# Fourteen groups of transposes through word copies, one tick later, in a decoder trunk on one core

## The chip, the core and the metric

The kernel runs on one core of one Trainium2 chip. The metric is the device time of one execution in microseconds (us); lower is better. Below, PE is TensorE's matmul stream, PEld its weight loads, DVE is VectorE, ACT is ScalarE, POOL is GpSimd and SP is SyncE. A transpose here is a matmul of a 128x128 block against an identity matrix; its result lands in PSUM, in banks of 128x512 fp32.

## The reference

Two layers of a decoder trunk over 256 tokens of width 2048: an attention mixer with latent projections (MLA), an MLP, a Mamba-2 mixer (SSM), an MLP, all in fp32. Cut to what matters:

```python
def rms_norm(x, g):
    y = xf * lax.rsqrt(jnp.mean(xf * xf, axis=-1, keepdims=True) + RMS_EPS)
    return y * g

def ssm_mixer(h, ...):                       # 8 groups of 512 channels
    ...
    y = y.reshape(B, S, SSM_D_INNER) * jax.nn.silu(z)
    y = y.reshape(B, S, SSM_GROUPS, SSM_D_INNER // SSM_GROUPS)
    y = y * lax.rsqrt(jnp.mean(y * y, axis=-1, keepdims=True) + RMS_EPS)
    return (y.reshape(B, S, SSM_D_INNER) * norm_g) @ w_out

for i in range(DEPTH):
    h = rms_norm(x, mix_norm_g[i])
    x = x + (mla_mixer(h, ...) if i % 2 == 0 else ssm_mixer(h, ...))
    h = rms_norm(x, mlp_norm_g[i])
    x = x + squared_relu_mlp(h, ...)
```

## The kernel before

All activations are held as two row tiles of 128 tokens (t = 0, 1) in quarters of 512 columns (nb = 0 to 3). To be a left-hand operand of the next matmul, a tile must be transposed. The kernel transposes a 128x512 tile by four PE transposes into one PSUM bank (`transposed`, L306 to L316), and then splits the bank into a rounded half `h` on ACT (L299) and the rest `lo` on DVE (L300); fp32r is the rounded format in which PE runs its large matmuls, and each fp32 product is made of three of them. Weights go the same way: an SP DMA brings 512 KB (`wraw`), ACT writes the rounded half `wh` (L102), DVE the rest `wl` (L103). Loads run six units ahead of PE and conversions three; a unit of an ordinary block is twelve matmuls of 512 columns.

PE's order is written out by hand: its instructions run as they are issued in the program. The order on the other engines comes from a planner, which fills each engine's queue by the order in the program and its own estimate of when operands are ready; every engine then runs its queue in order. What is to be put between matmuls is queued with `later(n, fn)`; `tick()` runs at the end of each weight key (24 matmuls in an ordinary block) and runs what is due. `later(0, fn)` runs at the next tick, `later(1, fn)` at the one after it.

Two kinds of places matter here:

- **Boundaries.** `finalize` (L382 to L403) adds a quarter of the residual (L399), multiplies it by the next norm's gain into a scratch tile `xg` (L401), squares it for the norm on ACT (L296), and queues the transposes of both row tiles with `later(0, ...)`. It is called for four quarters each after attention, after the first MLP and after the SSM. `by_tile` is true after attention and after the SSM.
- **Gated y.** In the SSM, `z_block(g)` makes the gate of group g from its matmuls; `gate` then multiplies on POOL (L1322), squares on ACT, makes the norm's factor (POOL, L283), writes the gated y of both row tiles into the scratch tiles `ws[t]` (DVE, L1328), and queues the eight transposes with `later(1, ...)`. Around them stand the group's products `y` on PE (L1291), which POOL (L1294, L1296) and DVE (L1297) take up, and `across` (L1243), a matmul of another group that uses the same two PSUM banks `sm` as the transposes.

Scratch tiles (`scratch()`, pool `s2`) share seven buffers. The MLPs already transpose most of their hidden tiles in the rounded form: `hidden` (L549 on) lets a POOL DMA copy the first three blocks of a tile into a tile `tr` of type fp32r (L559) and hands both to `transposed`, which takes blocks 0 to 2 from the copy with a rounded identity (L313) and block 3 from the fp32 source (L315). The copy leaves the words as they are; the type alone makes PE read them rounded. The rounded identity `identr` is cast on POOL at the start of each MLP from the identity in the tile of constants `cst`.

Of the kernel before, what the change touches and what calls it, by code (L numbers as in the profile page):

```python
# [20 lines left out]
F32 = mybir.dt.float32  # L21
F32R = mybir.dt.float32r
# [6 lines left out]
P = 128  # L29
# [9 lines left out]
NEG = -1.0e30  # L39
MAGIC = 12582912.0  # L40

C_ID, C_G0, C_GQ, C_GK, C_MQ, C_TRI, C_SEL = 0, 128, 144, 336, 528, 656, 784
C_INV, C_DTB, C_ALOG, C_CW, C_CB, C_END = 848, 880, 944, 1008, 1200, 1248


def inv_two_pi_parts():
# [168 lines left out]
class Trunk:  # L215
# [82 lines left out]
    def split_out(self, h, lo, src):  # L298
        self.nc.scalar.activation(h, src, AF.Copy)  # L299
        self.nc.vector.tensor_tensor(lo, src, h.bitcast(F32), ALU.subtract)  # L300

    def transposes(self, src, h, lo, t, wide=True):

        sl = slice(t * P, (t + 1) * P)
        self.transposed(src, h[:, :, sl], lo[:, :, sl], wide)

    def transposed(self, src, h, lo, wide=True):
        b = self.bank(wide)
        src, words = src if isinstance(src, tuple) else (src, None)
        for j in range(4):  # L310
            v = slice(j * P, (j + 1) * P)
            if words is not None and j < 3:
                self.nc.tensor.transpose(b.bitcast(F32R)[:, v], words[:, v], self.ident_r)  # L313
            else:
                self.nc.tensor.transpose(b[:, v], src[:, v], self.ident)  # L315
        self.split_out(h, lo, b.rearrange("p (k n) -> p k n", k=4))  # L316
# [67 lines left out]
    def finalize(self, nb, accs, wide=True):  # L384
        nc = self.nc
        g = self.gain_tile(self.nx_gain[nb])
        if not self.by_tile:
            self.nx[nb] = (self.ktile(self.xtp), self.ktile(self.xtp))
        elif nb % 2 == 0:
            for t in range(2):  # L390
                self.nx[nb // 2, t] = [self.ktile(self.xtp).rearrange("p a b -> p (a b)").rearrange("p (k n) -> p k n", n=P)
                                       for _ in range(2)]
        for t in range(2):
            if self.by_tile:
                h, lo = (v[:, 4 * (nb % 2):4 * (nb % 2) + 4] for v in self.nx[nb // 2, t])
            else:
                h, lo = (v[:, :, t * P:(t + 1) * P] for v in self.nx[nb])
            x = self.x[t][nb]
            nc.vector.tensor_tensor(x, accs[t], x, ALU.add)  # L399
            xg = self.scratch()  # L400
            nc.vector.tensor_tensor(xg, x, g, ALU.mult)  # L401
            self.square_sum(x, self.nx_ssq[:, t * 4 + nb:t * 4 + nb + 1])
            self.later(0, lambda h=h, lo=lo, xg=xg: self.transposed(xg, h, lo, wide))  # L403

    def boundary_end(self):

# [20 lines left out]
    def start(self, seq):  # L427
        nc, d = self.nc, self.d
        self.flow = Flow(nc, self.wp, seq, (6, 3))
        cst = self.c.tile([P, C_END], F32, name="cst")  # L430
        self.cst = cst
        self.ident = cst[:, C_ID:C_ID + P]
        self.mhalf = self.c.tile([P, 16], F32, name="mhalf")
        warm = self.s2.tile([P, 512], F32R, tag="s2", name="warm")
        nc.vector.memset(warm.bitcast(F32), 1.0)
        bank = self.sm.tile([P, 512], F32, tag="sm", name="warmed")
        for _ in range(WARM):
            nc.tensor.matmul(bank, warm[:, :P], warm, start=True, stop=True)
        nc.gpsimd.memset(self.mhalf, -0.5)
        nc.scalar.dma_start(cst[:, C_G0:C_GQ], d["cst"][:, C_G0:C_GQ])  # L440
        nc.scalar.activation(self.stat(1), self.mhalf[:, :1], AF.Copy)
        raws = [self.ktile(self.k4, F32) for _ in range(4)]
        parts = [(0, slice(k, k + 1)) for k in range(4)] + [(1, slice(0, 2)), (1, slice(2, 4)), (2, slice(0, 4)), (3, slice(0, 4))]

        def some_x():
            j, k = parts.pop(0)
            nc.sync.dma_start(raws[j][:, k], d["xT"][j][:, k])

        self.flow.load(2, ((0, 512), (512, 1024)), some_x)
        for u in range(3, 7):  # L450
            some_x()
            self.flow.load(u)
        self.pos = self.c.tile([P, 2], I32, name="pos")
        self.x = [[self.res.tile([P, 512], F32, name=f"x{t}{n}") for n in range(4)] for t in range(2)]

        self.rs_pool = [self.c.tile([P, 4], F32, name=f"rs{i}") for i in range(2)]
        self.phase = 0
        self.xT = [(self.ktile(self.xtp), self.ktile(self.xtp)) for _ in range(4)]

        def split_x(j, ks):  # L460
            h, lo = self.xT[j]
            for k in ks:
                g = cst[:, C_G0 + 4 * j + k:C_G0 + 4 * j + k + 1]
                if (j, k) == (0, 0):
                    nc.vector.tensor_scalar(h[:, k], raws[j][:, k], g, None, ALU.mult)
                else:
                    nc.scalar.activation(h[:, k], raws[j][:, k], AF.Copy, scale=g)
                nc.vector.scalar_tensor_tensor(lo[:, k], raws[j][:, k], g, h[:, k].bitcast(F32), ALU.mult, ALU.subtract)  # L468

        split_x(0, (0,))  # L470
        self.flow.convert(1)
        split_x(0, (1, 2))
        self.flow.convert(2)
        split_x(0, (3,))
        self.flow.load(7)
        nc.sync.dma_start(cst[:, :C_G0], d["cst"][:, :C_G0])
        nc.sync.dma_start(cst[:, C_GQ:], d["cst"][:, C_GQ:])
        nc.sync.dma_start(self.pos, d["pos"])
        split_x(1, range(4))
        ssq = self.stat(8)  # L480
        self.later(0, lambda: split_x(2, range(4)))
        self.later(1, lambda: split_x(3, range(4)))

        def stats(n):
            for t in range(2):
                nc.sync.dma_start(self.x[t][n], d["x"][t * P:(t + 1) * P, n * 512:(n + 1) * 512])
                self.square_sum(self.x[t][n], ssq[:, t * 4 + n:t * 4 + n + 1])
            if n == 3:
                self.set_rstd(ssq)

        for n, at in enumerate(X_AT):
            self.later(at, lambda n=n: stats(n))
# [51 lines left out]
    def mlp_body(self, mp, layer, gain):  # L544
        nc = self.nc
        xa, rs = self.xT, self.rs
        us = {}
        self.ident_r = mp.tile([P, P], F32R, name="identr")
        nc.gpsimd.tensor_copy(self.ident_r, self.ident)  # L549

        def hidden(r, pp, j, t):

            nc.scalar.activation(r, r, AF.Square)
            if (pp, j) not in us:
                us[pp, j] = (self.ktile(self.k4), self.ktile(self.k4))
            h, lo = us[pp, j]
            if pp in WORDS:
                q = mp.tile([P, 384], F32R, tag="tr", name=self.name("tr"), bufs=4)
                nc.gpsimd.dma_start(q.bitcast(F32), r[:, :384])  # L559
                r = (r, q)  # L560
            return lambda wide: self.transposes(r, h, lo, t, wide)

        def relu(src, t):
# [14 lines left out]
        at = [0.0, 0.0]  # L578
# [10 lines left out]
        def turn(r, p, j, t, us):  # L589

            fn = hidden(r, p, j, t)
            at[1] = max(at[0] + us + (COPY if p in WORDS else 0), at[1] + TR_GAP)
            due.append((at[1], lambda: fn(False)))

        def pair_of_banks(pool):
# [49 lines left out]
        for tok in tokens:  # L645
            key = (tok[0], layer) + tok[1:]
            if tok[0] == "s":
                _, p, name, d = tok
# [3 lines left out]
                if count.setdefault(name, 0) % 4 == 0:  # L652
                    pool = self.sm if name == "N7" else self.acc
# [7 lines left out]
            elif tok[0] == "c":  # L661
                _, p, j, o = tok
# [11 lines left out]
            else:  # L674
                _, p, nb, o = tok
# [373 lines left out]
    def ssm_body(self, sp, dp, gain):  # L1049
# [12 lines left out]
        xg = [None] * GROUPS  # L1062
# [241 lines left out]
        def z_block(g):  # L1304
# [11 lines left out]
            def gate():  # L1316
                if g not in ready:
                    self.later(0, gate)
                    return
                for t in range(2):  # L1320
                    x = xg[g][t]
                    nc.gpsimd.tensor_tensor(x, ws[t], x, ALU.mult)  # L1322
                    self.square_sum(x, ssq[:, t:t + 1], scale=rs[t])
                rr = self.rsqrt(ssq, 2, 512, 4 * EPS)
                r = self.stat(2)
                nc.vector.tensor_tensor(r, rr, rs2, ALU.mult)
                for t in range(2):
                    nc.vector.scalar_tensor_tensor(ws[t], xg[g][t], r[:, t:t + 1], ng, ALU.mult, ALU.mult)  # L1328
                    self.later(1, lambda t=t: self.transposes(ws[t], yT[g][0], yT[g][1], t, False))
                self.later(1, lambda: gated.add(g))  # L1330

            self.later(1, gate)

# [4 lines left out]
        for step in SSM_ORDER:  # L1338
# [18 lines left out]
            else:  # L1357
# [12 lines left out]
HEAD_BACKLOG = 4  # L1370
SSM_ORDER = ["B0", "d0", "C0", "x0", "B1", "x1", "C1", "x2", "z0", "x3", "z1", "x4", "z2", "o0", "x5", "z3", "x6", "z4", "o1",
             "x7", "z5", "z6", "o2a", "z7", "o2b", "o3"]


B12 = "raw"
# [1 line left out]
LATE5 = ()  # L1377
TR = (10, 8, 7, 7, 5)
TR_GAP = 4
WORDS = range(1, 7)  # L1380
COPY = 8
PAUSE = 2.7


# [192 lines left out]
```

## Time and profile before

| | us |
|---|---|
| median of 3 runs | 2288.92 |
| lowest and highest run | 2287.88, 2289.85 |
| the profiled execution, time | 2289.32 |
| the profiled execution, span of its trace | 2287.5 |

The span goes from the first to the last instruction; the time has 1.8 us around it. The profile gives busy time and share of the span for each engine, the granted PE clock in tenths for 40 slices of the span, and the chain of work that ended last. Views in order of time give start (us from the span's start), duration, engine, line of the kernel, operation, the tile written and the tiles read, the shapes, and how many instructions a row merges; a bracket holds the engine's idle time before the row and what ended it. PE's durations overlap, since matmuls are pipelined: the distance between starts is what a matmul costs in the stream. A view by tile gives, for each group, the least, median and largest duration in ns. A view of windows gives busy time of PE, PEld, DVE, ACT and POOL with the number of instructions, then PE's clock, the busy share of the DMA engines and GB/s.

### The profile page before, as it was taken

The page shows a single profiled execution, that of the slowest core. Times are in us where ns is not written, and L with a number is a line of the kernel's source. Part 1 is how long each engine was busy: PE and PEld are TensorE (multiplying, and loading weights), DVE is VectorE, ACT ScalarE, POOL GpSimd, SP SyncE. Part 2 cuts the span into 40 slices and gives each one's busy share as a digit, 9 for nine tenths or more (in the row PEclk, how much of TensorE's full clock was granted, in tenths as well). Part 3 has the DMA queues.
Part 4 walks back from the last instruction along what each step waited for, and adds up shares of the span by engine and source line. Part 5 has one row for each costly group of instructions (what it writes and reads, how often), then busy time and mean ns, then how long its engine had stood idle before and what let it go on. Part 6 is the DMA issues. An engine that isn't in the chain of part 4 may idle for free.

```text
span 2287.5 us, 30624 instructions
## 1 busy us (share of the span) xinstructions
PE 2280.0 (100%) x10929; PEld 1893.7 (83%) x10929; DVE 1906.0 (83%) x2318; ACT 1391.2 (61%) x1947; POOL 243.0 (11%) x279
## 2 busy tenths in 40 slices
PE   9999999999999999999999999999999999999999
PEld 7898888888888888888888888888888888888887
DVE  7785698999898897687888688676989989989985
ACT  7775476566566666564666555544666666666663
POOL 1430000000000000000133112110000000000000
PEclk9999999999999999999999999999999999999999
DMA  8435678888888878667877777666688888888875
GB/s 316 151 125 152 202 228 266 261 257 267 265 253 259 268 231 271 202 207 241 279 270 261 251 265 259 221 200 202 208 266 240 267 269 253 261 277 244 267 230 161
DMA packets 164985, 547.52 MB, mean 239 GB/s; under 512 B 18448, under 2 KB 27600, under 8 KB 163808
## 3 DMA queue, kind: packets, MB, share of 16 engines
q1 hardware_dynamic: 151264, 502.44, 66.4%
q0 software_dynamic: 11168, 38.85, 9.0%
q10 hardware_dynamic: 2400, 4.27, 0.5%
q8 instruction: 86, 1.41, 0.2%
q14 instruction: 67, 0.55, 0.1%
HBM read 529.65 MB, written 6.41 MB: 234 GB/s over the span
## 4 chain that ended last, share of the span: by engine, by line
PE 95%; DVE 2%; DMA 2%; ACT 1%; issue 1%; POOL 0%; SPq 0%; ACTq 0%; DVEq 0%
PE acc L330 13%; PE acc L331 13%; PE acc L334 13%; PE yp L606 9%; PE yp L607 9%; PE yp L605 9%; PE st L606 7%; PE st L607 7%; PE st L605 7%; DMA wraw<-mi 1%; PE sm L315 1%; DVE wl L103 1%; PE y L1291 1%; PE acc L607 1%; PE acc L605 1%
## 5 line engine op out<-in xcount | busy, mean ns | idle before, releaser
L102 ACT ACTIVATE wh<-wraw 128x1024 fp32r<-128x1024 f32 (+1 forms) x818 | 856.7, 1053 | 582.3 <-PE acc L331 287.9
L103 DVE TENSOR_TENSOR wl<-wraw,wh 128x1024 fp32r<-128x1024 f32 (+1 forms) x818 | 983.3, 1219 | 230.8 <-ACT wh L102 221.8
L605 PE MATMUL yp<-wh,k 128*128 128x512 f32 x896 | 349.3, 390 | 0.0
L607 PE MATMUL yp<-wh,k 128*128 128x512 f32 x896 | 349.1, 390 | 0.0
L606 PE MATMUL yp<-wl,k 128*128 128x512 f32 x896 | 348.9, 389 | 0.0
L330 PE MATMUL acc<-wh,xt 128*128 128x512 f32 x704 | 279.2, 397 | 1.0 <-ACT wh L102 1.0
L331 PE MATMUL acc<-wh,xt 128*128 128x512 f32 x704 | 274.6, 390 | 0.3 <-DVE xt L468 0.3
L102 ACT ACTIVATE wh<-wrx 128x1024 fp32r<-128x1024 f32 x168 | 177.8, 1058 | 153.7 <-PE yp L607 102.9
L103 DVE TENSOR_TENSOR wl<-wrx,wh 128x1024 fp32r<-128x1024 f32 x168 | 204.1, 1220 | 36.4 <-ACT wh L102 35.5
L606 PEld LDWEIGHTS yp<-wl,k 128*128 128x128 f32 x896 | 168.2, 188 | 35.1 <-DVE wl L103 0.4
L607 PEld LDWEIGHTS yp<-wh,k 128*128 128x128 f32 x896 | 168.2, 188 | 35.1
L605 PEld LDWEIGHTS yp<-wh,k 128*128 128x128 f32 x896 | 168.3, 188 | 34.7
L330 PE MATMUL acc<-wh,k 128*128 128x512 f32 x496 | 196.6, 396 | 0.0
L331 PE MATMUL acc<-wh,k 128*128 128x512 f32 x496 | 193.2, 390 | 0.0
L334 PE MATMUL acc<-wl,xt 128*128 128x512 f32 x704 | 188.3, 389 | 0.0
L605 PE MATMUL st<-wh,xt 128*128 128x512 f32 x448 | 177.4, 396 | 0.0
L607 PE MATMUL st<-wh,xt 128*128 128x512 f32 x448 | 174.9, 390 | 0.0
L606 PE MATMUL st<-wl,xt 128*128 128x512 f32 x448 | 174.9, 390 | 0.0
L330 PEld LDWEIGHTS acc<-wh,xt 128*128 128x128 f32 x704 | 132.2, 188 | 29.8 <-ACT wh L102 1.9
L331 PEld LDWEIGHTS acc<-wh,xt 128*128 128x128 f32 x704 | 132.3, 188 | 28.5 <-issue 1.2
L334 PEld LDWEIGHTS acc<-wl,xt 128*128 128x128 f32 x704 | 132.2, 188 | 27.6
L334 PE MATMUL acc<-wl,k 128*128 128x512 f32 x496 | 132.7, 389 | 0.0
(311 smaller groups left out, 3399.4 us busy)
## 6 DMA issues: line engine op xcount, KB each, us to landing
wraw<-mi SPq DMA_DIRECT2D x256, 512.0 KB, 5.5
wraw<-mo SPq DMA_DIRECT2D x256, 512.0 KB, 5.4
wraw<-si SPq DMA_DIRECT2D x160, 512.0 KB, 4.9
wraw<-so SPq DMA_DIRECT2D x64, 512.0 KB, 4.8
wrx<-mi SPq DMA_DIRECT2D x56, 512.0 KB, 5.1
wrx<-mi POOLq DMA_DIRECT2D x56, 512.0 KB, 7.6
wraw<-wo SPq DMA_DIRECT2D x32, 512.0 KB, 4.2
taps<-xD SPq DMA_DIRECT2D x16, 768.0 KB, 8.6
```

The source lines that it names most:

```text
L102: self.last = nc.scalar.activation(h[:, v], raw[:, v], AF.Copy)
L103: self.last_lo = nc.vector.tensor_tensor(lo[:, v], raw[:, v], h[:, v].bitcast(F32), ALU.subtract)
L315: self.nc.tensor.transpose(b[:, v], src[:, v], self.ident)
L330: nc.tensor.matmul(accs[t][:, :n], ah, wh[:, q, :], start=first and kt + q == 0, stop=False)
L331: nc.tensor.matmul(accs[t][:, :n], al, wh[:, q, :], start=False, stop=False)
L334: nc.tensor.matmul(accs[t][:, :n], lhs(kt + q, t)[0], wl[:, q, :], start=False, stop=en and q == nk - 1)
L605: nc.tensor.matmul(b, ah, wh, start=first and q == 0, stop=False)
L606: nc.tensor.matmul(b, ah, wl, start=False, stop=False)
L607: nc.tensor.matmul(b, al, wh, start=False, stop=last and q == 1)
L1291: nc.tensor.matmul(y[t][c, o], part(t)[:, c], xg[g][t][:, o], start=True, stop=True)
```

## The change

A helper `words` copies the first n blocks of a scratch tile by a POOL DMA into another buffer (of the MLP's pool in the MLPs, else of the scratch pool), and `transposed` takes as many blocks from the copy as there are. It is now also used for the gated y of every group other than group 5 (`SOON`), and at boundaries for quarters with `nb < 3 - by_tile`: 0 and 1 after attention and after the SSM, 0 to 2 after the first MLP. Both row tiles of such a group are copied, four blocks for t = 0 and three for t = 1, and the transposes (and the mark that the group is gated) run one tick later. Seven of the eight blocks are so transposed in rounded form; that makes the results of these transposes less exact. The rounded identity is made once at the start from an input of its own. In the MLPs the same tiles are copied as before.

```diff
-C_ID, C_G0, C_GQ, C_GK, C_MQ, C_TRI, C_SEL = 0, 128, 144, 336, 528, 656, 784
+C_G0, C_GQ, C_GK, C_MQ, C_TRI, C_SEL = 0, 16, 208, 400, 528, 656
...
+    def words(self, src, n, pool=None):
+
+        if pool:
+            q = pool.tile([P, n * P], F32R, tag="tr", name=self.name("tr"), bufs=4)
+        else:
+            q = self.s2.tile([P, 512], F32R, tag="s2", name=self.name("tr"))[:, :n * P]
+        self.nc.gpsimd.dma_start(q.bitcast(F32), src[:, :n * P])
+        return src, q, n
...
     def transposed(self, src, h, lo, wide=True):
         b = self.bank(wide)
-        src, words = src if isinstance(src, tuple) else (src, None)
+        src, words, n = src if isinstance(src, tuple) else (src, None, 0)
         for j in range(4):
             v = slice(j * P, (j + 1) * P)
-            if words is not None and j < 3:
+            if j < n:
                 self.nc.tensor.transpose(b.bitcast(F32R)[:, v], words[:, v], self.ident_r)
             else:
                 self.nc.tensor.transpose(b[:, v], src[:, v], self.ident)
...
-            self.later(0, lambda h=h, lo=lo, xg=xg: self.transposed(xg, h, lo, wide))
+            early = nb < 3 - self.by_tile
+            if early:
+                xg = self.words(xg, 4 - t)
+            self.later(int(early), lambda h=h, lo=lo, xg=xg: self.transposed(xg, h, lo, wide))
...
-        self.ident = cst[:, C_ID:C_ID + P]
+        self.ident_r = self.c.tile([P, P], F32R, name="ident")
+        self.ident = self.ident_r.bitcast(F32)
...
-        nc.sync.dma_start(cst[:, :C_G0], d["cst"][:, :C_G0])
+        one = self.scratch()
+        nc.sync.dma_start(one[:, :P], d["one"])
+        nc.gpsimd.tensor_copy(self.ident_r, one[:, :P])
...
-        self.ident_r = mp.tile([P, P], F32R, name="identr")
-        nc.gpsimd.tensor_copy(self.ident_r, self.ident)
...
-            if pp in WORDS:
-                q = mp.tile([P, 384], F32R, tag="tr", name=self.name("tr"), bufs=4)
-                nc.gpsimd.dma_start(q.bitcast(F32), r[:, :384])
-                r = (r, q)
+            if by_words(pp, j, t):
+                r = self.words(r, 3, mp)
...
-                    self.later(1, lambda t=t: self.transposes(ws[t], yT[g][0], yT[g][1], t, False))
-                self.later(1, lambda: gated.add(g))
+                    w = ws[t] if g == SOON else self.words(ws[t], 4 - t)
+                    self.later(1 + (g != SOON), lambda t=t, w=w: self.transposes(w, yT[g][0], yT[g][1], t, False))
+                self.later(1 + (g != SOON), lambda: gated.add(g))
...
+SOON = 5
...
-WORDS = range(1, 7)
...
+def by_words(p, j, t):
+
+    return 0 < p < 7
```

More of the change, by code (lines that the diff above doesn't have):

```diff
@@ L40 @@
 MAGIC = 12582912.0
-C_ID, C_G0, C_GQ, C_GK, C_MQ, C_TRI, C_SEL = 0, 128, 144, 336, 528, 656, 784
-C_INV, C_DTB, C_ALOG, C_CW, C_CB, C_END = 848, 880, 944, 1008, 1200, 1248
+C_G0, C_GQ, C_GK, C_MQ, C_TRI, C_SEL = 0, 16, 208, 400, 528, 656
+C_INV, C_DTB, C_ALOG, C_CW, C_CB, C_END = 720, 752, 816, 880, 1072, 1120
 def inv_two_pi_parts():
@@ L591, in turn @@
             fn = hidden(r, p, j, t)
-            at[1] = max(at[0] + us + (COPY if p in WORDS else 0), at[1] + TR_GAP)
+            at[1] = max(at[0] + us + (COPY if by_words(p, j, t) else 0), at[1] + TR_GAP)
             due.append((at[1], lambda: fn(False)))
@@ L1564 @@
     cw = f(ssm_conv_w)[0].reshape(4, 48, P).transpose(2, 1, 0).reshape(P, 192)
+    a["one"] = np.eye(P, dtype=np.float32)
     a["cst"] = np.ascontiguousarray(np.concatenate([
-        np.eye(P, dtype=np.float32), f(mix_norm_g)[0].reshape(16, P).T, rep(f(mla_qk_norm_q)[0]), rep(f(mla_qk_norm_k)[0]),
+        f(mix_norm_g)[0].reshape(16, P).T, rep(f(mla_qk_norm_q)[0]), rep(f(mla_qk_norm_k)[0]),
         upper * np.float32(NEG), np.triu(one), sel, rep(inv), rep(f(ssm_dt_bias)[0]),
```

## The prediction

> **What bounds the kernel now.** I read the page first, then the chain of waits, then TensorE's order of time around three groups of transposes, then the engines that feed them.
>
> ```profile
> span 2287.5 us, 30624 instructions
> PE 2280.0 (100%) x10929; PEld 1893.7 (83%) x10929; DVE 1906.0 (83%) x2318; ACT 1391.2 (61%) x1947; POOL 243.0 (11%) x279
> PEclk9999999999999999999999999999999999999999
> PE 95%; DVE 2%; DMA 2%; ACT 1%; issue 1%; POOL 0%; SPq 0%; ACTq 0%; DVEq 0%
> ```
>
> TensorE (PE) is busy all the time at the full granted clock, and the chain that ended last is PE for 95%. So a nanosecond taken off PE's own stream comes off the time, unless a new wait takes it back. The question is what a transpose costs in that stream. Three views in order of time, columns start, duration, engine, line, operation: a group of eight fp32 transposes between ordinary matmuls, a group of three rounded ones and one fp32 in the MLP, and the weight loads of both.
>
> ```profile
> 1164.41 1.07 PE L334 MATMUL acc<-wl,xt 128*128 128x512 f32 x4
> 1165.32 1.03 PE L315 MATMUL sm<-cst,s 128*128 128x128 f32 x8
> 1166.11 0.48 PE L330 MATMUL acc<-wh,xt 128*128 128x512 f32 x1
> 1166.66 0.39 PE L330 MATMUL acc<-wh,xt 128*128 128x512 f32 x1
> ...
> 407.53 0.39 PE L606 MATMUL yp<-wl,k 128*128 128x512 f32 x1
> 407.99 0.37 PE L313 MATMUL sm<-identr,tr 128*128 128x128 f32 x3
> 408.20 0.30 PE L315 MATMUL sm<-cst,s 128*128 128x128 f32 x1
> 409.03 0.39 PE L605 MATMUL st<-wh,xt 128*128 128x512 f32 x1
> ...
> 1165.32 0.79 PEld L315 LDWEIGHTS sm<-cst,s 128*128 128x128 f32 x7
> 408.00 0.22 PEld L313 LDWEIGHTS sm<-identr,tr 128*128 128x128 f32 x2
> 408.16 0.14 PEld L315 LDWEIGHTS sm<-cst,s 128*128 128x128 f32 x1
> ```
>
> Durations overlap; starts count. Four ordinary matmuls take 1165.32 - 1164.41 = 0.91 us, 0.227 each. From 1164.41 to 1166.66 is 2.25 us and holds six ordinary ones (1.36): **the eight fp32 transposes add 0.89 us**, 0.109 apart (the seven loads show it: (0.79 - 0.14)/6 = 0.108). From 407.53 to 409.03 is 1.50 us and holds five ordinary ones (1.13): **three rounded and one fp32 add 0.37 us**.
>
> What one more rounded transpose costs is the disputed number. The three start within 0.21 us, before the fourth. But their loads stand further apart than the first starts: two loads of 0.14 us fill 0.22, so the second begins 0.08 after the first, and the next at 408.16 again 0.08 later, while an ordinary matmul before the group hid the first load. In a longer run the load sets the pace: I take 0.083 us. The lower bound is 0.06 (0.21 us for three steps, the last at the load's pace of 0.08 or a little more); the upper bound is fp32's own 0.109.
>
> **The sum.** The diff changes the seven groups of gated y other than `SOON` (eight transposes each) and the quarters with `nb < 3 - by_tile`: two after attention, three after the first MLP, two after the SSM. I count seven quarters, so 14 groups, each now four rounded (t=0), then three rounded and one fp32 (t=1), back to back. One group then adds 0.37 + 4 x 0.083 = 0.70 us instead of 0.89. That saves 0.19 us, **14 x 0.19 = 2.7 us**. At 0.06 it would be 14 x 0.28 = 3.9, at 0.109 14 x 0.08 = 1.2.
>
> The Trainium skill, "TensorE: Matmul & The Clock Gate", section "Back-to-back issue gap", gives about 81 ns per matmul for a stream of loads and matmuls with 128 columns, and 56 ns for isolated matmuls of that width. The loads' 0.08 us side with the first; by it I estimate 14 x 0.20 = 2.8 us, by the second 14 x 0.29 = 4.0 us.
>
> **The copies.** Each group adds two POOL DMAs from SBUF to SBUF, 256 KB and 192 KB, 28 in all. Rows of the copies that the MLPs have already, then the gate of group 0 and the tightest gate, group 3:
>
> ```profile
> L559 POOL DMA_DIRECT2D tr<-s x48: 536/552/590, 364.1 to 2150.1; - x48
> DMA to landing us min/median/max: 2.1/5.1/7.2
> ...
> 1159.47 0.74 DVE L1328 SCALAR_TENSOR_TENSOR s<-xtm,st,gb 128x512 f32<-128x512 f32 x1
> 1159.84 6.25 POOL L1294 TENSOR_TENSOR xtm<-xtm,gb 128x512 f32<-128x512 f32 x2 [2.95 <-PE y L1291]
> 1166.17 1.62 POOL L1296 TENSOR_TENSOR xtm<-xtm,far 128x512 f32<-128x512 f32 x1
> ...
> 1349.49 0.75 DVE L1328 SCALAR_TENSOR_TENSOR s<-xtm,st,gb 128x512 f32<-128x512 f32 x1
> 1352.88 0.81 PE L315 MATMUL sm<-cst,s 128*128 128x128 f32 x6
> ```
>
> Queued behind a copy that waits for its source on POOL are L1294 and L1296, and DVE's L1297 waits for those. In group 0 the second copy would hold L1294 from 1159.84 to about 1160.8, 1 us; its result is next needed by the gate eight ticks later, so I charge 0 for it and let DVE's side of it count with the banks below. A tick in the SSM and at a boundary is one key of 24 matmuls, 24 x 0.227 = 5.44 us. In group 3 the second half of the gated y is ready at 1350.24 and its transposes move from 1352.88 to about 1358.3, so the copy has 8.1 us; group 0 has 1170.8 - 1160.2 = 10.6. An issue (0.55, inside the landing or ahead of it) and a landing of 5.1 fit, and even 0.55 + 7.2 = 7.8 does. `SOON`, group 5, with 2.7 us, is not moved. At the boundaries:
>
> ```profile
> 222.89 1.28 DVE L401 TENSOR_TENSOR s<-x,gb 128x512 f32<-128x512 f32 x2
> 227.16 0.60 PE L315 MATMUL yp<-cst,s 128*128 128x128 f32 x4
> ...
> 229.62 1.28 DVE L401 TENSOR_TENSOR s<-x,gb 128x512 f32<-128x512 f32 x2
> 233.49 0.60 PE L315 MATMUL yp<-cst,s 128*128 128x128 f32 x4
> ```
>
> Sources are ready at 224.17 and 230.90, the moved transposes due at about 232.6 and 238.9: 8.4 and 8.0 us. The other quarters follow the same pattern of two ticks. Hidden too, but with under 1 us to spare at the slowest landing seen: I charge 0 and keep 14 x 0.3 = 4.2 us as its bound. The copies carry 14 x 448 KB = 6.4 MB, 1.2% of what is moved. At the 266 GB/s of the row below that is 24 us of transfer if nothing hid it; the weights are loaded six units of 2.72 us ahead, so I charge nothing.
>
> ```profile
> 1157.00:1179.00 22.00, 22.00 (x155) 17.99 (x154) 19.49 (x31) 13.21 (x27) 9.29 (x4) 1.00 0.81 266
> ```
>
> **Scratch slots.** `words` takes its copy from the seven scratch buffers. At a gate there live at most two sources, two copies, two tanh tiles and one weighted x, seven, and the first source goes when its copy has landed. Where two quarters finish one tick apart (after attention, at the end of the SSM) the first leaves three or four slots taken, and the second wants four and two short-lived ones: it fits with a wait of about a Square (0.6 us) ahead of the last copy. Nothing on PE is due then, charged 0. The identity's move to the start takes one cast off each MLP, off the chain.
>
> **The rivals.**
>
> *The copies stand behind POOL's long products (slower).* POOL runs its queue in order. In group 0 the second source is ready at 1160.21, 0.37 us after L1294 could start. If both L1294 and L1296 are queued ahead of the copy, it issues at 1167.8 and lands at 1172.9 or, at 7.2, 1175.0; PE wants it at 1171.0. Groups 0, 1, 2 and 4 have this neighbour: 4 x 1.9 to 4 x 4.0 = 7.6 to 16 us, net 2294 to 2302. It decides when the issue is later than about 1165.9; one L1294 ahead (to about 1163) is harmless. Against it: in program order the copy comes first. For it: only readiness by the planner's costs, not by these rows, sets the order.
>
> *The banks come free too late (slower or about even).* The views of vector and tensor work behind groups 0 and 2:
>
> ```profile
> 1173.22 1.27 DVE L300 TENSOR_TENSOR k<-sm,k 128x512 fp32r<-128x512 f32 x2
> 1177.09 1.02 PE L1243 MATMUL sm<-s,cb 128*128 128x512 f32 x2
> ...
> 1261.12 1.03 PE L315 MATMUL sm<-cst,s 128*128 128x128 f32 x8
> 1267.10 1.28 DVE L300 TENSOR_TENSOR k<-sm,k 128x512 fp32r<-128x512 f32 x2
> 1270.01 2.35 DVE L103 TENSOR_TENSOR wl<-wraw,wh 128x1024 fp32r<-128x1024 f32 x2
> 1271.98 1.07 PE L334 MATMUL acc<-wl,k 128*128 128x512 f32 x4
> ...
> DVE xtm L1297 <- POOL xtm L1294: 10.7, 7, 2.0
> ```
>
> Both `sm` banks hold a group until L300 has read them; the next user, L1243, comes two ticks after the transposes now and one tick after them with the change. DVE reads group 0's first bank 8.5 us after the transposes start (1173.86 against 1165.32). The same lag from 1170.8 ends at 1179.3, L1243 would wait 2.4 us; group 1 looks like it, group 2 lags 6.6 us (to 1273.2, 0.5 us late), group 4 like it, group 3 less. Sum 5.8 us, net 2292.1, and more if DVE falls back further: it waits in order for POOL's products (last row), which copies can delay by an issue or two of 0.55, and in group 2 a weight half is done at 1271.2, only 0.8 us before PE takes it. Against it: the lag is DVE's backlog up to 1173.2, not the transposes' own, and 1173 is still before the moved L1243.
>
> The Trainium skill, "SBUF — State Buffer", section "A bandwidth-pool intuition that's wrong (but worth ruling out)", speaks against the change: a GpSimd-issued DMA of some 620 ns took some 3100 beside a VectorE copy that held the port they share, since its descriptors waited. The 48 copies here issue in 536 to 590 ns with DVE busy 83%, so the trace shows no sign of it; by that rule I estimate that a pair of copies would be 5 us later and miss the tight ticks.
>
> *The short pace holds (faster).* If rounded transposes go on at 0.06, 3.9 us: 2285.0. *A stall elsewhere goes too:* with 1 us beyond that, 2284. *The change gives nothing:* rounded ones in a long run at fp32's pace and late landings eat the 1.2 us: 2288.9.
>
> **How the numbers follow.** The profiled execution took 2289.32 us for its span of 2287.5; the median is 2288.92 and the runs go from 2287.88 to 2289.85. The sum 2289.32 - 2.7 = 2286.6 in that execution is 2286.3 by the median. Chances: the forecast 40%, the short pace 20%, a stall gone too 7%, banks 16%, POOL's queue 13%, nothing gained 4%. 0.2% is 4.6 us, about what a measurement can tell from no change, so below 2284.3 counts as faster: 7% and two fifths of the short pace, 15%. Above 2293.5: POOL's queue and some of the banks' 16%, 19%. The rest, 66%, is within. The range from 2283.5 to 2294 takes in the short pace and the banks and leaves out most of POOL's queue and a rest at both ends, some 18%; the likeliest case alone is 2285 to 2287.7, from the two bounds of the pace.
>
> **What would show it.** Each step right: L315 falls by 98 transposes, and 98 of the rounded form appear beside the MLPs' 144; a group of eight adds 0.70 us between ordinary matmuls, its loads 0.08 apart; no PE row waits for a DMA of a copy; L1243 starts in step with the matmuls before it. Wrong: loads 0.06 apart (2285); a gap on PE ahead of a group, with the copy's issue behind L1294 or landing after the tick; a gap ahead of L1243 with L300 later than it; new rows in which PE waits for L103 near 1272 and 1412. A span more than 4.6 us off with none of these would mean that the rearranged order of the other engines, not the edits, set it.

## The result and the profile after

| | before | after |
|---|---|---|
| median, us (6 runs each) | 2289.6 | 2303.53 |
| lowest and highest run | 2287.88, 2289.86 | 2300.07, 2306.68 |
| profiled execution, time and span | 2289.32, 2287.5 | 2300.07, 2298.0 |

After against before: 1.0060, 95% interval 1.0049 to 1.0071. The change makes the kernel slower by 14 us; the profiled execution, the fastest of the six, by 10.75. The page of the changed kernel hardly shows why:

```profile
span 2298.0 us, 30746 instructions
PE 2283.8 (99%) x10929; PEld 1892.3 (82%) x10929; DVE 1910.2 (83%) x2318; ACT 1392.9 (61%) x1947; POOL 256.1 (11%) x306
PEclk9999999999999999999999999999999999999999
PE 45%; DVE 1%; ACT 0%; DMA 0%; issue 0%; SPq 0%; DVEq 0%; ACTq 0%
```

PE's busy time rose by 3.8 us with the same 10929 matmuls, 98 of them cheaper, and the span by 6.7 us more than that. So there are waits, and matmuls that last longer. The view of waits of the changed kernel says whose (us in total, times, longest); before had no row like the first:

```profile
PE sm L1254 <- DVE k L300: 7.8, 4, 3.9
PE warmed L451 <- DVE warm L448: 1.4, 1, 1.4
PE acc L343 <- DVE wl L103: 1.0, 2, 0.6
```

L1254 is `across` (L1243 before). The order of time on PE around group 1 of the changed kernel holds all that happened to the forecast:

```profile
1218.07 1.07 PE L343 MATMUL acc<-wl,xt 128*128 128x512 f32 x4
1218.97 0.71 PE L322 MATMUL sm<-ident,tr 128*128 128x128 f32 x7
1219.52 0.29 PE L324 MATMUL sm<-ident,s 128*128 128x128 f32 x1
1219.57 0.48 PE L339 MATMUL acc<-wh,xt 128*128 128x512 f32 x1
1219.89 0.39 PE L340 MATMUL acc<-wh,xt 128*128 128x512 f32 x1
1220.12 0.40 PE L339 MATMUL acc<-wh,xt 128*128 128x512 f32 x1
...
1230.42 2.05 PE L1254 MATMUL sm<-s,cb 128*128 128x512 f32 x2 [3.85 <-DVE k L300]
1231.48 1.42 PE L339 MATMUL acc<-wh,xt 128*128 128x512 f32 x1
1232.69 0.63 PE L340 MATMUL acc<-wh,xt 128*128 128x512 f32 x1
1233.12 0.63 PE L339 MATMUL acc<-wh,xt 128*128 128x512 f32 x1
...
1235.68 1.46 PE L343 MATMUL acc<-wl,xt 128*128 128x512 f32 x4
1236.97 0.40 PE L339 MATMUL acc<-wh,xt 128*128 128x512 f32 x1
```

**The pace is as forecast.** From 1218.07 to 1220.12 are 2.05 us with six ordinary matmuls (1.36): the group adds 0.69 us, where eight fp32 ones added 0.89. In the next matmuls a little of that 0.20 us is made up: from the fourth matmul ahead of a group to the eighth behind it the medians are 3.39 us before and 3.21 after, 0.18 us less, which is 2.5 us in 14 groups. The experiments below reckon with that.

**Then `across` waits 3.85 us for L300**, and after it matmuls start 0.43 us apart instead of 0.227. The window from 1229 to 1237 us of the changed kernel (busy time of PE, PEld, DVE, ACT and POOL, then PE's clock, DMA share, GB/s) shows that the granted clock is 0.57, and two rows of before give the normal length of the same matmuls:

```profile
1229.00:1237.00 8.00, 6.58 (x15) 4.54 (x16) 5.37 (x8) 4.07 (x6) 0.00 (x0) 0.57 0.93 284
```

```profile
1224.65 1.02 PE L1243 MATMUL sm<-s,cb 128*128 128x512 f32 x2
...
1228.28 0.39 PE L330 MATMUL acc<-wh,xt 128*128 128x512 f32 x1
```

From `across` to the first matmul of the next weight unit are 1236.97 - 1230.42 = 6.55 us after, 1228.28 - 1224.65 = 3.63 before: 2.9 us lost to the slow clock. In tenths of full speed over 57 us, as on the page, it does not show.

**The account.** PE's last matmul ends 10.6 us later than before; with the 2.5 us gained, 13 us were lost on balance. The losses lie between 1170 and 1440 us, where PE goes from 1.4 us ahead of the kernel before to 11.4 behind it. Waits of `across` 7.8 (four: groups 0, 1, 2 and 4, with 1.4, 3.9, 1.7 and 0.9), slow clock 2.9, waits for weight halves 1.0 make 11.7. Most of the rest lies around the waits: over each of them the starts are some 0.17 us further apart than the idle time and one matmul, and the next two starts 0.07 us or more. Why L300 is late, VectorE's order of time shows, first of the changed kernel (group 0, then group 1), then of `e5_words_on_time` below, which transposes group 0 at the old tick and stands here for the old order:

```profile
1171.81 2.18 DVE L1287 SCALAR_TENSOR_TENSOR mt<-mt,dt,cb 128x128 f32<-128x128 f32 x8
1173.91 2.35 DVE L103 TENSOR_TENSOR wl<-wraw,wh 128x1024 fp32r<-128x1024 f32 x2
1176.18 1.28 DVE L300 TENSOR_TENSOR k<-sm,k 128x512 fp32r<-128x512 f32 x2
...
1225.22 2.18 DVE L1287 SCALAR_TENSOR_TENSOR mt<-mt,dt,cb 128x128 f32<-128x128 f32 x8
1227.32 2.35 DVE L103 TENSOR_TENSOR wl<-wraw,wh 128x1024 fp32r<-128x1024 f32 x2
1229.60 1.28 DVE L300 TENSOR_TENSOR k<-sm,k 128x512 fp32r<-128x512 f32 x2
```

```profile
1172.86 1.28 DVE L300 TENSOR_TENSOR k<-sm,k 128x512 fp32r<-128x512 f32 x2
1174.06 2.18 DVE L1287 SCALAR_TENSOR_TENSOR mt<-mt,dt,cb 128x128 f32<-128x128 f32 x8
1176.15 2.35 DVE L103 TENSOR_TENSOR wl<-wraw,wh 128x1024 fp32r<-128x1024 f32 x2
```

At the old tick L300 stands ahead of eight products of the heads (L1287, 2.18 us) and two weight halves (2.35 us); a tick later the planner puts it behind them. The transposes moved by a tick (5.4 us), `across` did not. Before the change `across` of group 0 started 3.2 us after L300 had read the first bank. In the changed kernel L300 has read it 7.5 us after the group's first transpose starts, against 8.6 before. So the lag gave back 1.1 us of the 5.4, the margin of 3.2 us is used up, and `across` waits. In groups 1, 2 and 4 the lag itself grew, from 8.6, 6.7 and 6.8 us to 11.3, 8.1 and 7.1.

### The profile page after: what moved, and what is told of

Same layout as the page of the kernel before. It is cut to its first block, busy times and chain, and to the rows that moved or that the text cites. A ratio compares the mean times of both kernels' runs of the same rounds, so it can differ in the third digit from the quotient of the medians.

```text
span 2298.0 us, 30746 instructions
## 1 busy us (share of the span) xinstructions
PE 2283.8 (99%) x10929; PEld 1892.3 (82%) x10929; DVE 1910.2 (83%) x2318; ACT 1392.9 (61%) x1947; POOL 256.1 (11%) x306
## 5 line engine op out<-in xcount | busy, mean ns | idle before, releaser
L102 ACT ACTIVATE wh<-wraw 128x1024 fp32r<-128x1024 f32 (+1 forms) x818 | 857.9, 1054 | 581.2 <-PE acc L340 276.5
L103 DVE TENSOR_TENSOR wl<-wraw,wh 128x1024 fp32r<-128x1024 f32 (+1 forms) x818 | 985.3, 1221 | 235.6 <-ACT wh L102 224.2
L102 ACT ACTIVATE wh<-wrx 128x1024 fp32r<-128x1024 f32 x168 | 178.0, 1059 | 152.8 <-PE yp L618 97.0
L103 DVE TENSOR_TENSOR wl<-wrx,wh 128x1024 fp32r<-128x1024 f32 x168 | 204.4, 1221 | 38.2 <-ACT wh L102 37.0
L339 PEld LDWEIGHTS acc<-wh,xt 128*128 128x128 f32 x704 | 133.3, 189 | 29.4 <-ACT wh L102 1.0
L616 PE MATMUL st<-wh,sN 128*128 128x512 f32 x336 | 133.0, 396 | 0.0
```

The lines of the kernel that those rows point to most:

```text
L102: self.last = nc.scalar.activation(h[:, v], raw[:, v], AF.Copy)
L103: self.last_lo = nc.vector.tensor_tensor(lo[:, v], raw[:, v], h[:, v].bitcast(F32), ALU.subtract)
L339: nc.tensor.matmul(accs[t][:, :n], ah, wh[:, q, :], start=first and kt + q == 0, stop=False)
L616: nc.tensor.matmul(b, ah, wh, start=first and q == 0, stop=False)
```

## The experiments

All times are medians; ratios are against the kernel before on the same chip, with 95% intervals. Differences are against the changed kernel unless said otherwise.

**`across` a tick later.**

```diff
-                self.later(1, across)
+                self.later(2, across)
```

> The changed kernel with one number altered: the product `across` is queued two ticks after its weighted x instead of one, so it again stands two ticks behind the transposes that were moved. Theory A (the loss is `across` waiting for the two `sm` banks until VectorE's L300 has read them, plus the slower clock after the longest of these waits): the gaps of 1.76, 4.25, 2.08 and 1.28 us ahead of L1254 go or fall below 0.5 us each, the clock stays at 1.00 throughout, and the time falls by about 12 us to 2286-2290 us. Rival B (the copies, by POOL, the SBUF or VectorE's delay, slow the SSM and L1254 only shows it): the waits move to another instruction and the time stays at 2297-2304 us. Rival C (the backlog of VectorE is the limit, and whatever is due next on PE waits): part is won, 2292-2297 us, with waits for the products' y or for `far` instead.

Measured 2292.52 us, ratio 1.0013 (1.0004 to 1.0022). No PE row waits for L300 any more, but one new wait stands near 1204 us, for a weight half, with a granted clock of 0.50 until 4.8 us after it:

```profile
PE acc L343 <- DVE wl L103: 2.2, 1, 2.2
```

Theory A was right on the gaps and too hopeful on the time. The time is in rival C's range, though the wait is not for what rival C named.

**Boundaries alone.** The gates go back to fp32 transposes at the old tick without copies.

> The seven gates are put back as before (fp32 transposes, one tick after the gate, no copies); the seven boundary quarters keep the changed form. Theory A (the loss is in the SSM's gates alone, and the boundaries give 0.18 us a group): 7 x 0.18 = 1.3 us faster than before, 2287-2289 us, and no gap ahead of `across`. Rival B (the boundaries' copies or later transposes cost something too, hidden under the gates' loss): 2290-2293 us, with PE waits of the next stage's first matmuls for L300 at 298, 885 or 1620 us.

Measured 2289.02 us, 0.9995 (0.9986 to 1.0004), no wait of `across`. The loss is in the gates; the boundaries' gain, forecast as 1.3 us, is inside what can be told from nothing.

**The late tick without copies.** The gates' transposes are fp32 from their source, a tick later; the boundaries are as before.

```diff
-            early = nb < 3 - self.by_tile
+            early = False
...
-                    w = ws[t] if g == SOON else self.words(ws[t], 4 - t)
+                    w = ws[t]
```

> No copies and no rounded transposes at all: the gates' transposes stay fp32 from their source but come one tick later as in the changed kernel; the boundaries are as before. Theory A (the tick alone makes the loss): gaps ahead of L1254 for groups 0, 1, 2 and 4 like the changed kernel's, and 2297-2306 us, since the 2.5 us of the faster pace are missing too. Rival B (the copies make the loss): no gaps, 2288-2291 us.

Measured 2305.89 us, 1.0070 (1.0056 to 1.0084), with the same row of waits as the changed kernel:

```profile
PE sm L1254 <- DVE k L300: 7.8, 4, 3.9
PE acc L343 <- DVE wl L103: 3.7, 4, 1.2
```

The tick alone makes the loss. The changed kernel, with copies and rounded transposes, is about 2.4 us faster than this one, near the 2.5 of the pace, but the intervals of the two (1.0049 to 1.0071 and 1.0056 to 1.0084) overlap.

**The gates' transposes in `acc` banks.**

> The changed kernel, but the gates' moved transposes go to banks of the ring `acc` (those of the blocks' accumulators) and leave the two `sm` banks alone. Theory A (the two `sm` banks are what `across` waits for): no gap ahead of L1254; the time is 2286-2290 us, if the blocks do not then wait for `acc`. Rival B (copies): unchanged, 2297-2304 us. Rival C (VectorE's backlog limits through any bank): a block's first matmul waits for L300 on an `acc` bank in place of L1254, and the time is 2292-2304 us.

Measured 2311.53 us, 1.0089 (1.0074 to 1.0104). `across` waits no more, but the transposes themselves wait for their banks, 8.6 us for the residual's additions (L436) and 3.1 us for L1214, which read the blocks' sums out of `acc`; a block's matmul also waits 1.4 us for L300, as rival C had it. A miss: the new waits cover what the move takes away, so the run decides little between the theories.

**Copies, but the old tick.** Groups 0, 1, 2, 4 and 7, whose sources are ready early enough, use copies and rounded transposes at the old tick; 3, 5 and 6 stay fp32.

```diff
-                    w = ws[t] if g == SOON else self.words(ws[t], 4 - t)
-                    self.later(1 + (g != SOON), lambda t=t, w=w: self.transposes(w, yT[g][0], yT[g][1], t, False))
-                self.later(1 + (g != SOON), lambda: gated.add(g))
+                    w = self.words(ws[t], 4 - t) if g in EARLY else ws[t]
+                    self.later(1, lambda t=t, w=w: self.transposes(w, yT[g][0], yT[g][1], t, False))
+                self.later(1, lambda: gated.add(g))
...
-SOON = 5
+EARLY = (0, 1, 2, 4, 7)
```

> The changed kernel without the tick at the gates: all gates' transposes are queued one tick after the gate, as before; groups 0, 1, 2, 4 and 7, whose sources are ready 5 us and more before that tick, use word copies and the rounded form, groups 3, 5 and 6 stay fp32. The boundaries are as in the change. Theory A (the tick, not the copies, makes the loss): L300 keeps its place ahead of the heads' products on VectorE, no gap ahead of L1254, and 12 groups gain 0.18 us each: 2286.5-2288.5 us. Rival B (the copies slow POOL, VectorE or the loads): 2291 us or more, with waits for L103 or L300. Rival C (the copies land too late for the early tick): PE waits at L322 for the copies' DMA, some us in all, 2289-2296 us.

Measured 2287.15 us, 0.9992 (0.9983 to 1.0001): 1.8 us under the kernel before, where 12 groups of 0.18 make 2.2. No PE wait for a copy or ahead of `across`. It is the fastest kernel of the study; by the interval it is not shown to be faster than before. It shows that the tick was not needed for most groups: the copies of its gates and last boundary land in 2.9 us in the median, at most 4.9, and in the kernel before group 0 had 5.1 us from its source to its transposes.

**Copies that nothing reads**, with fp32 transposes at the old tick.

> The seven gates issue their copies, but nothing reads them: the transposes are fp32 from the source at the old tick. The boundaries are as in the change. Theory A (copies cost nothing): as with the gates put back, 2288-2290 us, no gap ahead of L1254. Rival B (copies slow the SSM by themselves): 2293-2300 us.

Measured 2288.78 us, 0.9997 (0.9988 to 1.0006). That is what the boundaries alone gave (0.9995): the copies cost nothing that can be measured.

**The heads' products behind L300** in VectorE's queue.

```diff
-                nc.vector.scalar_tensor_tensor(half(t), half(t), dt[:, t, h:h + 1], cb[g][:, 256 * t:256 * t + P],
-                                               ALU.mult, ALU.mult)
+                with self.tc.issue_after(self.cut.ins):
+                    nc.vector.scalar_tensor_tensor(half(t), half(t), dt[:, t, h:h + 1], cb[g][:, 256 * t:256 * t + P],
+                                                   ALU.mult, ALU.mult)
```

> The changed kernel, with one edge in VectorE's queue: the heads' products (L1287 of the change) are queued behind the L300 that was issued last ahead of them. Theory A (what makes L300 late is the work that stands ahead of it in VectorE's queue, eight products of 2.18 us and two weight halves of 2.35): L300 moves ahead of most products, the four gaps shrink by 1 to 2.2 us each, the one of 4.25 us below 2.5 and with it the stretch at the slow clock; 2292-2298 us. Rival B (L300 is late because its own bank or ACT's half is late, not for its place): the gaps stay and the time is 2300 us or more.

Measured 2306.17 us, 1.0074 (1.0060 to 1.0088). The waits of `across` did shrink, from 7.8 us to 4.7 (group 0's is gone, the longest is 1.8), and that step of theory A holds. The time did not follow: waits for weight halves rose from 1.0 us to 9.0 (6.4 on L103, 2.6 on L102). The forecast was wrong, and this is the first sign of a second cause.

**Group 1 put back** (fp32, old tick).

> The changed kernel with group 1's gate alone put back (fp32, old tick, no copy). Theory A: of the loss only group 1's part goes, 4.0 us of waiting and, if the slow clock behind it belongs to the long wait, 3.1 us more: 2303.5 - 7.1 + 0.2 = 2296.6 us; the gaps of groups 0, 2 and 4 stay at 1.3 to 2.1 us. Rival (the slow clock has another cause): 2299.5 us, or the slow stretch turns up behind another gap of under 2.5 us. Rival (the waits share one backlog, so that taking one away lengthens the next): 2300 us or more.

Measured 2299.62 us, 1.0043 (1.0029 to 1.0057), 3.9 less than the changed kernel where 7.1 were forecast. Group 1's gap is gone, those of 0, 2 and 4 stay; new ones came, 3.6 us for weight halves (L103) and 1.2 us for the gated y itself (L1339). The time and the trace are as the first rival had them: the slow clock turned up behind group 2's wait of 1.7 us, which follows a wait of 1.5 us. Taking the long wait away does not take the slow clock away.

**One `sm` bank left free.** Of the gates' two banks one comes from the ring `yp`.

```diff
-                    self.later(1 + (g != SOON), lambda t=t, w=w: self.transposes(w, yT[g][0], yT[g][1], t, False))
+                    self.later(1 + (g != SOON), lambda t=t, w=w: self.transposes(w, yT[g][0], yT[g][1], t, g != SOON))
```

> The changed kernel, but of the two banks of a gate's transposes one comes from the ring `yp` (that of the products y) and one from `sm`, so that one of the two `sm` banks stays free for `across`. Theory A (`across` waits only because both `sm` banks are held): the gaps ahead of L1254 vanish or stay under 0.5 us although L300 runs as late as in the change, and 10 us or so come back: 2289-2295 us, with what is left in waits for weight halves (L103). Rival B (VectorE's lateness costs the same in any case): the wait moves to another first user of a bank (L1302 or L1254) or of a weight half, 2298 us or more.

Measured 2299.15 us, 1.0043 (1.0029 to 1.0057). Its view of waits:

```profile
PE acc L343 <- DVE wl L103: 6.4, 5, 1.8
PE acc L339 <- ACT wh L102: 3.8, 4, 1.5
```

Every wait of `across` is gone although L300 is as late as ever, so the held banks are the cause of those waits. But 10.2 us stand at weight halves instead: rival B is right on the sum. The banks are only the first thing that VectorE's lateness meets. How much is met next differs: with `across` later, where no bank is waited for either, only one wait of 2.2 us for a weight half came up. No run shows why it is so much more here.

**Group 1 alone, then group 0 alone, a tick later**, all else as in `e5_words_on_time`.

> The kernel with word copies and the old tick at the gates (groups 0, 1, 2, 4 and 7 in the rounded form), with group 1's transposes alone a tick later. It was 2287.2 us without that tick. Theory A1 (each group's wait is its own): a gap of about 4 us ahead of L1254 near 1224 us and 3 us at the slow clock behind it, 2294 us. Theory A2 (the long wait of group 1 in the change was built up by group 0's late tick ahead of it): a gap of 1.5 to 2.5 us, no slow clock, 2289-2290 us.

> The same with group 0's transposes alone a tick later. Theory A1: a gap of 1.5 us ahead of L1254 near 1175 us and nothing else, 2288.7 us. Theory A2 (group 0's tick also disorders what follows): beside the 1.5 us waits for weight halves (L103) near 1204 to 1224 us that the kernel before does not have, 0.5 to 2.6 us, in all 2289.5-2292 us.

Measured 2292.96 us (1.0014, 1.0005 to 1.0024) and 2295.15 us (1.0026, 1.0015 to 1.0036). Each has a gap of 1.3 us at its own `across`; group 1's wait of 3.9 us at `across` and the slow clock behind it are absent, so they were built up behind group 0's late tick (A2). But each costs 6 to 8 us against 2287.15, more than A2 allowed, and most of it later: group 0's tick makes group 1's transposes wait 2.7 us for their copy, whose source is late, with a granted clock of 0.50 until 3.9 us after it, and group 1's costs a wait of 2.1 us for a weight half near 1274 us. What happens in between, the queues of SP, ScalarE and VectorE, one after the other, show, first of `e5_words_on_time` and then of `e11_only_group0`:

```profile
1173.34 0.45 SPq L1280 DMA_DIRECT2D cm<-cumD  x1
1173.88 0.42 SPq L390 DMA_DIRECT2D gb<-sng  x1
1174.35 0.93 SPq L1280 DMA_DIRECT2D cm<-cumD  x2
1177.39 1.47 SPq L85 DMA_DIRECT2D wraw<-si  x2
...
1188.60 1.25 ACT L1322 ACTIVATE s<-acc,rs 128x512 f32<-128x512 f32 x2
...
1189.87 1.28 DVE L1323 SCALAR_TENSOR_TENSOR s<-s,acc 128x512 f32<-128x512 f32 x2
```

```profile
1172.47 0.42 SPq L1280 DMA_DIRECT2D cm<-cumD  x1
1172.99 0.47 SPq L390 DMA_DIRECT2D gb<-sng  x1
1175.33 1.46 SPq L85 DMA_DIRECT2D wraw<-si  x2
1176.89 0.92 SPq L1222 DMA_DIRECT2D taps<-xD  x2
1179.97 3.20 SPq L85 DMA_DIRECT2D wraw<-si  x3
1183.21 1.02 SPq L1280 DMA_DIRECT2D cm<-cumD  x2
...
1191.27 0.99 ACT L1284 ACTIVATE mt<-cm,pcum 128x128 f32<-128x128 f32 x3 [4.61 <-DMA cm<-cumD]
...
1194.17 1.25 ACT L1322 ACTIVATE s<-acc,rs 128x512 f32<-128x512 f32 x2
...
1192.60 1.36 DVE L1287 SCALAR_TENSOR_TENSOR mt<-mt,dt,cb 128x128 f32<-128x128 f32 x4 [4.68 <-ACT mt L1285]
...
1195.44 1.28 DVE L1323 SCALAR_TENSOR_TENSOR s<-s,acc 128x512 f32<-128x512 f32 x2
```

The planner moved two loads of the heads' rows `cm` behind five weight loads in SP's queue, from 1174.35 to 1183.21 us. ScalarE then waits 4.61 us for them in order, with a weight half and the next gate's tanh (L1322) behind, and VectorE 4.68 us for ScalarE. The gate's work comes 5.6 us later, and VectorE has idle time where it had work before. ScalarE does not wait longer for `cm` in all: from 1150 to 1450 us it is 24.3 us in the first kernel and 24.7 in the second (25.8 before the change, 25.4 after). What changed is where the wait falls: VectorE's waits for the heads' exponentials rose from 2.3 to 5.6 us (from 1.3 to 5.1 with the change). Its busy time from 1180 to 1200 us, from the view of windows, tells the kernels with group 0's late tick from those without, all but the last of the table:

| kernel | VectorE busy, us of 20 |
|---|---|
| before; copies at the old tick | 18.11; 18.69 |
| group 1 alone late (group 0 at the old tick) | 18.24 |
| changed; group 0 alone late | 12.40; 12.20 |
| `across` later; one `sm` bank free; heads' products behind | 10.90; 11.46; 13.80 |
| below, `cm` by POOL: changed; with one `sm` bank free | 14.31; 17.25 |

With group 1 alone late the dip comes one group later: 12.70 us from 1220 to 1240, where `e5_words_on_time` has 17.20. So the disorder follows the moved transposes. But it does not set the time by its size: `across` later has the least in the table, 10.90, and took 2292.52 us.

**`cm` loaded by POOL's queue**, in the changed kernel, with one `sm` bank free as well, and as a control with the copies at the old tick.

```diff
-            nc.sync.dma_start(cm, cumD[h:h + 1].to_broadcast([P, S]))
+            nc.gpsimd.dma_start(cm, cumD[h:h + 1].to_broadcast([P, S]))
```

> The changed kernel with the heads' rows of cumulated sums (cm) loaded by POOL's DMA queue instead of SP's, so that they no longer stand behind weight loads. Theory A3 (the late tick does its harm by two ways, the two sm banks and cm loads that come late behind weight loads on SP): ScalarE's waits for cm fall, the waits for weight halves near 1204 us go, group 0's gap at `across` of about 1.5 us stays, groups 1 and 2 fall to about that too; 2293-2297 us. Rival (VectorE's backlog is general and cm is only where it shows): 2300 us or more.

> The changed kernel with both: one bank of the gates' transposes from `yp`, and cm loaded by POOL. Theory A3: neither way of harm is left; no gap ahead of L1254, VectorE's wait for the heads' exponentials under 3 us in all, no PE waits for weight halves between 1200 and 1290 us; 2286-2290 us. Rival (general backlog): waits for weight halves stay, 2296 us or more.

> The control: the kernel with word copies at the old tick (2287.2 us) with cm loaded by POOL. If that move neither helps nor harms by itself, 2286-2289 us; if POOL's long products delay cm there, 2290 us or more, and the two runs beside it cannot be read as tests of SP's order.

Measured 2307.03 us (1.0070, 1.0051 to 1.0088), 2290.44 us (1.0005, 0.9996 to 1.0015) and 2295.11 us (1.0027, 1.0016 to 1.0038). With both, the late tick costs no more than can be told from nothing, though the time is 0.4 us above the forecast range: `across` does not wait, and weight halves cost PE 2.0 us in the whole span. The views of waits, first with `cm` alone moved, then with both:

```profile
PE sm L1254 <- DVE k L300: 10.0, 4, 3.5
```

```profile
PE acc L343 <- DVE wl L103: 1.3, 2, 1.0
PE acc L339 <- ACT wh L102: 0.7, 1, 0.7
```

With `cm` alone moved, the waits of `across` grew from 7.8 to 10.0 us and ScalarE's waits for `cm` did not fall (29.4 us from 1150 to 1450): the first forecast failed, and the bank wait stands by itself. The control was not neutral, 8 us slower than without the move, with 5.2 us of waits for weight halves near 1271 and 1416 us; loading by POOL has a price of its own and another order. By the control's own condition the other two cannot be read as tests of SP's order.

What stands is this. With the bank freed alone some 10 us of loss remained, with `cm` moved alone some 18, and with both none that can be told from nothing. So a kernel with all late ticks need not lose time, and the held banks are one part of the loss. That the other part is VectorE's disorder fits the traces, but is argued; that the position of `cm` on SP is its source is not shown.

## Why the prediction was wrong

**Right.** The pace: 0.70 us for a group was forecast, 0.69 measured. The page of the Trainium skill "TensorE: Matmul & The Clock Gate", section "Back-to-back issue gap", has 81 ns per matmul for a stream of loads and matmuls with 128 columns. In the 14 groups the seven rounded transposes start 0.076 us apart, near that and above the 0.06 of the short pace. The copies: charged 0, and with copies that nothing read no cost showed. POOL's queue as a rival: false. This view of POOL in the changed kernel shows both copies of group 0 ahead of L1305 (L1294 before), and groups 1, 2 and 4 have the same order:

```profile
1158.20 0.63 POOL L308 DMA_DIRECT2D tr<-s  x1 [2.75 <-issue]
1159.35 0.54 POOL L308 DMA_DIRECT2D tr<-s  x1 [0.52 <-DVE s L1339]
1159.91 4.76 POOL L1305 TENSOR_TENSOR xtm<-xtm,gb 128x512 f32<-128x512 f32 x2
```

Every copy of the changed kernel issued in 538 to 798 ns with VectorE busy 83%, so no issue looks like the 3100 ns of the Trainium skill's "SBUF — State Buffer", section "A bandwidth-pool intuition that's wrong (but worth ruling out)".

**The step that failed** is the one that counted a tick as time for the copy and as nothing else. The sum held no term for what the tick does to the two `sm` banks; that stood among the rivals with 16%. The runs show what that term is worth: `across` waits 7.8 us for L300 and matmuls at the slow clock behind the longest wait cost 2.9 us, and the same row of waits comes with the tick alone, without copies. The rival had place and mechanism right. It took L300's lag as fixed and so had 2.4, 2.4, 0.5 and 0.5 us for groups 0, 1, 2 and 4, 5.8 in all; measured are 1.4, 3.9, 1.7 and 0.9. What it held against itself was wrong: "the lag is DVE's backlog up to 1173.2, not the transposes' own" supposes that L300 keeps its place in VectorE's queue and is done at about 1173. It lost that place to 4.5 us of other work and started at 1176.18.

Two terms were missing altogether: the slow clock, and the idle time that a changed order in SP's, ScalarE's and VectorE's queues makes. In the changed kernel the second shows as 1.0 us at weight halves and, since group 1's wait is 3.9 us here and 1.3 with group 1 alone late, in the length of that wait; in the experiments it surfaces as late weight halves tens of us on. The prediction's last sentence named that kind of cause only for a span that none of its signs would explain.

**Open** is why the planner places `cm` later when only a gate's transposes move, and how much of the loss this move alone makes; since the control was not neutral, no run separates it from other shifts of order.

## What to carry to other kernels

Work moved by a slot on a busy engine takes its readers along: before charging zero for it, find who reads its result, what that reader stands behind in its in-order queue at the new time, and who needs the buffer next. Where a planner orders the other engines, compare their queues before and after, loads included; a small load that is moved behind large ones can idle an engine that has no time to spare. And check first that the delay is needed: here five of the seven moved groups had time for the copy at the old tick.

## What the runs showed of the hardware

A wait on PE costs more than itself once it is long. Of eleven PE waits of 2.2 us and more (2.6 us and more between two starts) in the changed kernel and the experiments, ten were followed by a granted clock of 0.50 that lasted until 2.9 to 6.3 us after the wait; one, of 2.8 us, was not. Of the shorter waits of 1.5 to 2.1 us none that stood alone was followed by it. Of six that came 0.8 us behind another wait of 0.6 us or more, four were (`e3_late_fp32`, `e7_heads_behind`, `e8_group1_back`, `e14_cm_by_pool`) and two were not, one each in `e7_heads_behind` and `e14_cm_by_pool`. So the length of a wait alone does not tell.

The changed kernel's runs spread over 6.6 us where the six of the kernel before spread over 2. Waits do not spread the times in every kernel: with one `sm` bank free, with 10.2 us of waits for weight halves, the runs lie within 1.5 us.
